# Two-layer hybrid decoder trunk on one core: layer 1's first heads put between the products of the query projections, early weight loads in halves, and turns moved in both output projections

## The chip, the cores and the metric

The kernel runs on one core of one Trainium2 chip. The metric is device time in microseconds (us), from runs of the whole kernel; smaller is better. A core has five engines that work through their own instruction streams in order and wait for each other through semaphores: TensorE (PE; its weight loads are listed as PEld), VectorE (DVE), ScalarE (ACT), GpSimd (POOL) and SyncE (SP). SP issues nearly all of the loads of this kernel. PSUM, where PE writes, is handed out in banks of 128 x 512 float32.

## The reference

The input is 256 tokens of 1024 channels, float32. Two layers follow each other, with a shared key/value step between them:

```python
hn = rms_norm(h, norm_gain[0, 0])                       # layer 0
h = h + stick_breaking_attention(hn, sb_w_qkv, sb_w_o)  # 16 heads of 64
h = h + sqrelu_mlp(rms_norm(h, norm_gain[0, 1]), w1, w2)  # 1024 -> 4096 -> 1024
shared = nsa_shared_kv(h, ...)     # one K/V projection for three branches
hn = rms_norm(h, norm_gain[1, 0])                       # layer 1
h = h + nsa_attention(hn, w_q, gate_b, w_o, shared)
h = h + sqrelu_mlp(rms_norm(h, norm_gain[1, 1]), w1, w2)
return rms_norm(h, final_norm)
```

Stick-breaking attention weighs a key by exp(log_sigmoid(z) + a reversed cumulative sum of log_sigmoid(-z)). The attention of layer 1 has 16 query heads in four groups that share keys and values. Each head is answered three times: over 15 compressed blocks (their keys and values come from a small MLP with 256 hidden units over 32 tokens each), over selected blocks of 64 tokens (with 256 tokens there are four blocks, all of which are selected, so this is causal attention), and over a window of 512 (causal attention again). The first 16 channels of queries and keys are rotated by position for the last two. Three sigmoid gates per head, columns of the query projection, weigh the three answers; their sum goes through the output projection.

## The kernel before

**Products.** Every large product is done in three passes of reduced-width float32 (`mm3`, lines 131 to 134, and `wide`, lines 139 to 145): each operand is split into a high part and the rest. Weights come through one stream: `feed` lists the tiles in the order of use, `fetch` (76) issues the next load into one of three `raw` buffers, and `split` (86) makes a high part `wh` on ACT (line 96) and a low part `wl` on DVE (line 97), each for half a tile at a time. `W(i)` makes sure that tile i is split, `step()` splits one more half, at most two tiles ahead. A load is issued when the second half of an earlier tile has been split. Most tiles are 128 x 2048 float32, 1 MB; the value projection of layer 0 is cut by `V_CUT` into six tiles: four with one block of 128 channels (512 KB), two with two blocks (1 MB). The first tile's load is two DMAs, one for each half of its columns.

**Layer 0.** The value projection (`v_proj`) goes block by block, as weights and input columns (`x_load`, `x_cut`) come in. Then eight query-key pairs (`proj`) run, with the attention of earlier pairs inside: `scores` (PE, then exponential, logarithm, scan, subtraction, and an exponential in line 432), `turn` (transposes in line 442, copies), `values`. The attention of the last pairs stands inside the output projection: `out_proj` takes a dictionary of steps that it calls at (i, n, kk), where i is the half of the 1024 input channels, n the half of the output columns (one weight tile for each i and n) and kk the block of 128 channels in that tile. A block of one tile is six products.

**Layer 1** (`nsa`, 470). `kv_proj` 0 to 2 make the keys and values of the three branches; `rope` (519) rotates on POOL in four instructions, for one tile of 128 tokens at a time; `keys_tr` transposes the keys; `cw_proj` is the first product of the compressing MLP, lines 612 to 623 its activation `hu`. `q_proj` (628) makes the queries in three parts (4, 6 and 6 heads, the gates with the first), each from two weight tiles with 24 products each; `mid` is called between the two tiles. `q_unrot` transposes unrotated queries for the compressed branch, `q_rope` rotates and splits, `q_rot` transposes the rotated ones. `cmp_kv` and `cmp_kv2` finish the compressed keys and values, `cmp_probs` makes compressed softmax weights for eight heads (one token tile after the other), `cmp_tr` transposes them. For each head, `scores` makes both branches' scores and exponentials, `scale` multiplies them on POOL by gate over sum, `turn` transposes, and `values` makes the answer of two heads. Lines 822 to 871 set the order: between the two tiles of parts 1 and 2 stand the transposes and rotation of the part before; after part 2, with no projection beside them, the scores of heads 1 to 3 and the rest of the preparation; then a loop over the heads, and the output projection with the last `values` inside.

**Order.** The order in which the source issues work is a priority. The order in each engine's stream is fixed at build time from it and from the expected readiness of inputs and buffers, so that a step can stand earlier or later than in the source. Tiles of one tag share a number of buffers: `bank` and `bank2` are two tags of four PSUM banks each, and a projection of layer 1 holds two of the first four.

## Time and profile before

| | |
|---|---|
| median of 3 runs | 640.27 us (639.65 to 640.73) |
| profiled execution | 642.27 us |
| its span, first to last instruction | 640.4 us |
| mean granted clock of PE | 0.999 |
| PE busy | 624.8 us (98%) |
| DVE busy | 435.6 us (68%) |
| ACT busy | 350.5 us (55%) |
| POOL busy | 59.6 us (9%) |
| weight subtractions on DVE, line 97 | 204, mean 1187 ns |
| weight casts on ACT, line 96 | 204, mean 1016 ns |
| HBM read | 106.22 MB |
| chain that ended last | PE 75%, DVE 12%, ACT 4%, DMA 4%, issue 3% |

A line of the timeline has the start from the span's start, the duration, engine, source line, operation, what is written from what, and in brackets the idle time before it and what ended it. Products overlap: one that is listed with 0.33 us can be followed by the next one 0.17 us later, and the busy time of PE counts the union. Layer 0 takes until about 122 us, its MLP until 302, the key/value step and layer 1's attention until 455, the last MLP the rest.

### The profile page before, as it was taken

The numbers are of one execution on the slowest core, as the hardware profiler recorded it, in microseconds if no ns is written. First come the engines' busy times: TensorE is split into PE (matmuls) and PEld (weight loads), VectorE is DVE, ScalarE is ACT, GpSimd is POOL, SyncE is SP. The second block draws the span as 40 slices with busy tenths as digits, with TensorE's granted clock in tenths as the row PEclk, the third lists the DMA queues.
The fourth block names the chain that finished last, engine by engine and source line by source line (L and its number), as shares of the span: only waits on it lengthen the run. The fifth ranks groups of instructions, "written<-read, shape, count | busy, mean of one in ns | idle before, by whom it ended". The sixth has DMA issues, their size and how long they took to land.

```text
span 640.4 us, 9068 instructions
## 1 busy us (share of the span) xinstructions
PE 624.8 (98%) x3541; PEld 527.9 (82%) x3541; DVE 435.6 (68%) x632; ACT 350.5 (55%) x606; POOL 59.6 (9%) x100
## 2 busy tenths in 40 slices
PE   9999999999999999999999999999999999999995
PEld 6799986888888888888889987777888888888884
DVE  5587887776566665666899879763776566666554
ACT  5666665464444544444847777752564544454433
POOL 0200000000000000000133344550000000000000
PEclk9999999999999999999999999999999999999999
DMA  8953333446555454553465742001545454555501
GB/s 264 409 211 133 132 132 121 151 174 212 197 182 206 160 208 169 201 190 133 150 253 192 258 156 98 3 2 66 198 168 205 162 204 182 198 198 197 198 0 67
DMA packets 17467, 107.86 MB, mean 168 GB/s; under 512 B 2320, under 2 KB 3088, under 8 KB 5648
## 3 DMA queue, kind: packets, MB, share of 16 engines
q1 hardware_dynamic: 16416, 106.03, 46.6%
q10 hardware_dynamic: 1008, 1.25, 0.5%
q8 instruction: 28, 0.46, 0.3%
q14 instruction: 15, 0.12, 0.1%
HBM read 106.22 MB, written 1.05 MB: 168 GB/s over the span
## 4 chain that ended last, share of the span: by engine, by line
PE 75%; DVE 12%; ACT 4%; DMA 4%; issue 3%; POOL 1%; SPq 0%; POOLq 0%; ACTq 0%; DVEq 0%
PE pu L137 27%; PE acc L132 11%; PE acc L133 11%; PE acc L134 11%; DVE wl L97 5%; PE po L137 2%; DMA raw<-in_wv 2%; DVE sbs L430 2%; PE pk L134 2%; PE pk L132 2%; PE pk L133 2%; ACT wh L96 1%; DVE sbe L424 1%; ACT sbs L429 1%; ACT sbs L428 1%
## 5 line engine op out<-in xcount | busy, mean ns | idle before, releaser
L97 DVE TENSOR_TENSOR wl<-raw,wh 128x1024 fp32r<-128x1024 f32 (+3 forms) x204 | 235.1, 1187 | 125.3 <-ACT wh L96 125.1
L96 ACT CAST wh<-raw 128x1024 fp32r<-128x1024 f32 (+3 forms) x204 | 198.5, 1016 | 118.2 <-PE acc L134 50.9
L137 PE MATMUL pu<-xn,wh 128*128 128x512 f32 x512 | 130.1, 392 | 0.6 <-DVE xn L204 0.6
L137 PEld LDWEIGHTS pu<-xn,wh 128*128 128x128 f32 x512 | 93.8, 188 | 19.6 <-DVE xn L204 1.8
L132 PE MATMUL acc<-wh,hh 128*128 128x512 f32 x256 | 100.2, 391 | 0.0
L133 PE MATMUL acc<-wl,hh 128*128 128x512 f32 x256 | 100.1, 391 | 0.0
L134 PE MATMUL acc<-wh,hl 128*128 128x512 f32 x256 | 99.5, 389 | 0.0
L137 PEld LDWEIGHTS pu<-xn,wl 128*128 128x128 f32 x512 | 71.0, 190 | 5.0
L137 PE MATMUL pu<-xn,wl 128*128 128x256 f32 x512 | 74.0, 282 | 0.0
L134 PEld LDWEIGHTS acc<-wh,hl 128*128 128x128 f32 x256 | 48.1, 188 | 10.6 <-DVE hl L293 0.4
L132 PEld LDWEIGHTS acc<-wh,hh 128*128 128x128 f32 x256 | 48.2, 188 | 9.6 <-ACT hh L292 0.6
L133 PEld LDWEIGHTS acc<-wl,hh 128*128 128x128 f32 x256 | 48.2, 188 | 8.8
L292 ACT CAST hh<-ms 128x512 fp32r<-128x512 f32 x32 | 19.9, 620 | 64.7 <-DVE ms L288 64.7
L286 ACT COPY mr<-pu 128x256 f32<-128x256 f32 x64 | 23.6, 369 | 29.2 <-PE pu L137 29.2
L132 PE MATMUL qk<-xa,wh 128*128 128x256 f32 x128 | 37.0, 289 | 0.0
L133 PE MATMUL qk<-xa,wh 128*128 128x256 f32 x128 | 36.2, 283 | 0.0
L134 PE MATMUL qk<-xa,wl 128*128 128x256 f32 x128 | 36.2, 283 | 0.0
L293 DVE TENSOR_TENSOR hl<-ms,hh 128x512 fp32r<-128x512 f32 x32 | 22.1, 692 | 19.9 <-ACT hh L292 19.9
L287 DVE TENSOR_TENSOR mu<-pu,mr 128x256 f32<-128x256 f32 x64 | 26.7, 418 | 5.8 <-ACT mr L286 5.8
L790 POOL TENSOR_TENSOR pe<-pe,rs 128x256 f32<-128x256 f32 (+1 forms) x32 | 27.1, 866 | 23.6 <-DVE rs L786 19.9
L132 PE MATMUL acc<-wh,oT 128*128 128x512 f32 x64 | 25.8, 403 | 0.0
L132 PEld LDWEIGHTS qk<-xa,wh 128*128 128x128 f32 x128 | 24.5, 191 | 1.0 <-issue 0.9
(187 smaller groups left out, 919.7 us busy)
## 6 DMA issues: line engine op xcount, KB each, us to landing
raw<-in_w SPq DMA_DIRECT2D x64, 1024.0 KB, 4.8
raw<-in_wqk SPq DMA_DIRECT2D x8, 1024.0 KB, 6.5
raw<-in_wo SPq DMA_DIRECT2D x8, 1024.0 KB, 4.8
raw<-in_wkv SPq DMA_DIRECT2D x6, 1024.0 KB, 4.8
raw<-in_cw SPq DMA_DIRECT2D x4, 1024.0 KB, 4.8
raw<-in_wv SPq DMA_DIRECT2D x2, 1024.0 KB, 8.1
raw<-in_wv SPq DMA_DIRECT2D x3, 512.0 KB, 5.6
raw<-in_wqb SPq DMA_DIRECT2D x2, 768.0 KB, 4.1
```

The source lines that it names most:

```text
L96: nc.scalar.copy(h[:, r], raws[j][:, r])
L97: nc.vector.tensor_sub(lo[:, r], raws[j][:, r], f32(h[:, r]))
L132: nc.tensor.matmul(o, a[0], b[0], start=first, stop=False, skip_group_check=True)
L133: nc.tensor.matmul(o, a[0], b[1], start=False, stop=False, skip_group_check=True)
L134: nc.tensor.matmul(o, a[1], b[0], start=False, stop=last, skip_group_check=True)
L137: nc.tensor.matmul(o, a, b, start=first, stop=last, skip_group_check=True)
L286: nc.scalar.copy(r[:, q], pu[f][:, 256:512])
L287: nc.vector.tensor_add(u[:, q], pu[f][:, 0:256], r[:, q])
L292: nc.scalar.copy(hh, sv)
L293: nc.vector.tensor_sub(hl, sv, f32(hh))
L430: nc.vector.tensor_tensor_scan(s[:, ::-1], s[:, ::-1], go_on[:, ::-1], 0.0, OP.add, OP.mult)
L790: nc.gpsimd.tensor_tensor(s, s, rs[:, t, :][:, :, None].to_broadcast([P, 2, n]), op=OP.mult)
```

## The change

Seven edits, in the order of the file. `fetch` makes two DMAs of each of the first seven loads (before: of the first alone). In layer 0's output projection `turn(NP - 2)` moves from (0, 0, 2) to (0, 1, 0) and `values(NP - 2)` from (0, 1, 1) to (0, 1, 2). `rope` takes both token tiles in its four instructions. `q_proj` takes a dictionary of steps by (i, kk) in place of `mid`, keeps both token tiles in one tile `q`, and makes the gates of both in one set of instructions. `cmp_probs` does the softmax of both token tiles together, from one PSUM bank. The last `values` of layer 1 writes a bank of the other tag. And the order of layer 1 is rewritten:

```diff
@@ fetch
-            if len(raws) == 1:
+            if len(raws) <= len(V_CUT) + 1:
@@ layer0
-        out_proj(oT, i_o0, {(0, 0, 2): [lambda: scores(NP - 1), lambda: turn(NP - 2), lambda: values(NP - 3)],
-                            (0, 1, 1): [lambda: values(NP - 2)],
+        out_proj(oT, i_o0, {(0, 0, 2): [lambda: scores(NP - 1), lambda: values(NP - 3)],
+                            (0, 1, 0): [lambda: turn(NP - 2)], (0, 1, 2): [lambda: values(NP - 2)],
@@ nsa
-        def rope(src, t, n):
...
+        def rope(src, n):
+
+            a = ap.tile([P, T, n, 16], F32, name="ropea", tag="ropea")
+            b = ap.tile([P, T, n, 16], F32, name="ropeb", tag="ropeb")
+            nc.gpsimd.tensor_mul(a, src[:, :, :, 0:16], cos[:, :, None, :].to_broadcast([P, T, n, 16]))
+            nc.gpsimd.tensor_mul(b[:, :, :, 0:8], src[:, :, :, 8:16], sin[:, :, None, 0:8].to_broadcast([P, T, n, 8]))
+            nc.gpsimd.tensor_mul(b[:, :, :, 8:16], src[:, :, :, 0:8], sin[:, :, None, 8:16].to_broadcast([P, T, n, 8]))
+            nc.gpsimd.tensor_add(src[:, :, :, 0:16], a, b)
...
-        def q_proj(n, mid=None):
+        def q_proj(n, hooks):
...
-                if i and mid is not None:
-                    mid()
                 for kk in range(4):
                     if kk % 2 == 0:
                         step()
+                    for f in hooks.get((i, kk), ()):
+                        f()
...
         def cmp_probs(hf):
+            pc = bank("psc")
             for t in range(T):
-                pc = bank("psc")
...
+            n = 8 * T
+            pv = pc[:, 0:T * 120].rearrange("p (h n) -> p h n", h=n)
...
-            po = bank("po1")
+            po = bank2("po1") if p == NP - 1 else bank("po1")
...
-        q1 = q_proj(1, after_q0)
-        q_rot(r[0], 0, 4)
-        cmp_kv2(*r.pop(1))
...
+        def turned(n, p0, np_, nh):
+            q_unrot(qn[n], p0, np_)
+            r[n] = q_rope(qn[n], nh)
+
+
+        qn[1] = q_proj(1, {(0, 1): [lambda: turned(0, 0, 2, 4)], (0, 2): [lambda: r.append(cmp_kv())],
+                           (1, 0): [lambda: q_rot(r[0], 0, 4)], (1, 1): [lambda: cmp_kv2(*r.pop())],
+                           (1, 2): [lambda: scores(0)]})
         qs[1] = big([P, NH // 2, T * P], F32R, "qs1")
-        scale(0)
-        scores(1)
-        q_rot(r[1], 4, 6)
-        q_unrot(q2, 5, 3)
-        r.append(q_rope(q2, 6))
-        cmp_probs(0)
-        scores(2)
-        scale(1)
-        turn(0)
-        cmp_tr(0)
-        q_rot(r[2], 10, 6)
+        qn[2] = q_proj(2, {(0, 1): [lambda: turned(1, 2, 3, 6), lambda: scores(1)], (0, 2): [lambda: scale(0)],
+                           (0, 3): [lambda: scores(2), lambda: scale(1)], (1, 0): [lambda: turn(0)],
+                           (1, 1): [lambda: q_rot(r[1], 4, 6), lambda: cmp_probs(0)],
+                           (1, 2): [lambda: turn(1), lambda: scale(2)], (1, 3): [lambda: scores(3)]})
...
-        scores(3)
-        scale(2)
-        turn(1)
-        cmp_probs(1)
-        for h in range(3, NH + 1):
+        cmp_tr(0)
+        for h in range(3, NH):
             if h + 1 < NH:
                 scores(h + 1)
-            if h < NH:
-                scale(h)
+            scale(h)
+            if h == 3:
+                turned(2, 5, 3, 6)
             if h % 2:
                 values((h - 3) // 2)
             turn(h - 1)
+            if h == 4:
+                q_rot(r[2], 10, 6)
+            if h == 5:
+                cmp_probs(1)
             if h == 6:
                 cmp_tr(1)
         xn = xt_tiles("n")
-        out_proj(oT, i_o1, {(0, 0, 2): [lambda: values(NP - 1)], (1, 1, 2): [lambda: xt_evac(xt_tr(0), 0, 3, xn)]})
+        out_proj(oT, i_o1, {(0, 0, 1): [lambda: turn(NH - 1)], (0, 0, 3): [lambda: values(NP - 1)], (1, 1, 2): [lambda: xt_evac(xt_tr(0), 0, 3, xn)]})
```

## Rows read from the trace of the kernel before

**Rows 1.** Waits of PE: who waited for whom, us in total, times, longest.
```profile
PE pv L132 <- ACT wh L96: 1.5, 1, 1.5
PE z L137 <- ACT pe L775: 1.4, 2, 0.7
PE pa L442 <- ACT sbe L432: 1.1, 2, 0.8
...
PE pct L745 <- DVE ce L737: 0.8, 1, 0.8
```

**Rows 2.** Stretches: length, then busy PE, PEld, DVE, ACT, POOL, clock, DMA.
```profile
354.20:376.70 22.50, 21.77 (x147) 20.88 (x146) 16.91 (x34) 13.60 (x27) 8.86 (x17) 1.00 0.62 222
376.70:392.00 15.30, 13.01 (x102) 10.56 (x102) 13.87 (x37) 14.06 (x49) 8.64 (x14) 1.00 0.18 70
```

**Rows 3.** Timeline of the first 20 us: PE, ACT, SP.
```profile
17.57 0.39 PE L134 MATMUL pv<-wh,xa 128*128 128x512 f32 x1
19.46 1.19 PE L132 MATMUL pv<-wh,xa 128*128 128x512 f32 x4 [1.50 <-ACT wh L96]
...
18.37 2.00 ACT L96 CAST wh<-raw 128x1024 fp32r<-128x1024 f32 x2 [2.70 <-DMA raw<-in_wv]
...
7.38 0.43 SPq L336 DMA_DIRECT2D xin<-in_xcols  x1
```

**Rows 4.** DMA issues from 0 to 40 us: count, KB each, us to landing.
```profile
raw<-in_wv SPq DMA_DIRECT2D x2, 1024.0 KB, 8.1
...
xin<-in_xcols SPq DMA_DIRECT2D x1, 512.0 KB, 6.6
```

**Rows 5.** Stretches as in group 2; the last number is GB/s.
```profile
4.00:6.00 2.00, 2.00 (x6) 0.75 (x5) 0.71 (x2) 1.36 (x3) 0.00 (x0) 1.00 0.98 245
...
12.00:14.00 2.00, 2.00 (x11) 1.65 (x10) 0.84 (x2) 1.19 (x3) 0.00 (x0) 1.00 0.96 328
```

**Rows 6.** Timeline of layer 0's output projection, ACT and PE.
```profile
97.25 0.85 ACT L432 ACTIVATE sbe<-sbe 128x774 f32<-128x774 f32 x1 [1.40 <-DVE sbe L431]
...
98.15 0.88 PE L442 MATMUL pa<-ident,sbe 128*128 128x128 f32 x6 [0.80 <-ACT sbe L432]
```

**Rows 7.** Timeline of the second query projection's first half, PE and DVE.
```profile
354.23 0.34 PE L132 MATMUL pq<-wh,xq 128*128 128x384 f32 x1
...
358.39 0.60 PE L660 MATMUL ptq<-ident,q 128*128 128x128 f32 x4
359.32 0.45 PE L693 MATMUL pht<-ident,hu 60*128 60x60 f32 x4 [0.33 <-DVE hu L623]
...
358.64 0.62 DVE L623 TENSOR_TENSOR hu<-hu,hx 60x512 f32<-60x512 f32 x1
```

**Rows 8.** Timeline of PE in the stretch of the first heads.
```profile
383.35 0.22 PE L137 MATMUL psc<-cmb,cbf 128*128 128x120 bf16 x1
383.37 0.36 PE L137 MATMUL z<-kT,qs 128*128 128x256 f32 x1
```

**Rows 9.** Timeline of the second key branch's rotation: POOL, DVE, PE.
```profile
339.24 1.33 POOL L524 TENSOR_TENSOR ropea<-kd,cst 128x128 f32<-128x128 f32 x1
...
343.17 0.46 POOL L529 TENSOR_TENSOR kd<-ropea,ropeb 128x128 f32<-128x128 f32 x1
...
338.78 4.13 DVE L97 TENSOR_TENSOR wl<-raw,wh 128x1024 fp32r<-128x1024 f32 x3
...
341.85 0.60 PE L573 MATMUL ptk<-ident,kd 128*128 128x128 f32 x4
...
343.68 0.66 PE L573 MATMUL ptk<-ident,kd 128*128 128x128 f32 x4 [0.87 <-POOL kd L529]
```

**Rows 10.** Query evacuations on DVE (timeline), and the page's group of the scaling.
```profile
354.43 0.53 DVE L480 TENSOR_SCALAR q<-pq,r 128x304 f32<-128x304 f32 x1
364.92 0.61 DVE L480 TENSOR_SCALAR q<-pq,r 128x384 f32<-128x384 f32 x1
...
L790 POOL TENSOR_TENSOR pe<-pe,rs 128x256 f32<-128x256 f32 (+1 forms) x32 | 27.1, 866 | 23.6 <-DVE rs L786 19.9
```

More of the change, by code (lines that the diff above doesn't have):

```diff
@@ L565, in keys_rope @@
         def keys_rope(br):
-            for t in range(T):
-                rope(kd[br][t].rearrange("p g a d -> p (g a) d"), t, 2 * NG)
+            rope(kdt[:, br].rearrange("p t (h d) -> p t h d", d=DH), 2 * NG)
         def keys_tr(br):
@@ L626, in nsa @@
         gates = ap.tile([P, T, 48], F32, name="gates")
-        def q_proj(n, mid=None):
+        def q_proj(n, hooks):
             cn = 384 if n else 304
-            qn = [ap.tile([P, 384], F32, name=f"q{t}", bufs=2)[:, 0:cn] for t in range(T)]
+            qn = ap.tile([P, T, 384], F32, name="q", bufs=2)
             pq = [bank(f"pq{t}") for t in range(T)]
@@ L642, in q_proj @@
             for t in range(T):
-                evac(qn[t], pq[t][:, 0:cn], t)
+                evac(qn[:, t, 0:cn], pq[t][:, 0:cn], t)
             if n == 0:
-                for t in range(T):
-                    gt = gates[:, t, :]
-                    nc.vector.tensor_add(gt, qn[t][:, 256:304], gbs)
-                    nc.vector.tensor_scalar(gt, gt, -80.0, None, op0=OP.max)
-                    nc.scalar.activation(gt, gt, AF.Exp, scale=-1.0)
-                    nc.vector.tensor_scalar(gt, gt, 1.0, None, op0=OP.add)
-                    nc.vector.reciprocal(gt, gt)
+                nc.vector.tensor_add(gates, qn[:, :, 256:304], gbs[:, None, :].to_broadcast([P, T, 48]))
+                nc.vector.tensor_scalar(gates, gates, -80.0, None, op0=OP.max)
+                nc.scalar.activation(gates, gates, AF.Exp, scale=-1.0)
+                nc.vector.tensor_scalar(gates, gates, 1.0, None, op0=OP.add)
+                nc.vector.reciprocal(gates, gates)
+                nc.vector.tensor_tensor(gates[:, :, 0:NH], gates[:, :, 0:NH],
+                                        cst[:, C_ANY:C_ANY + T][:, :, None].to_broadcast([P, T, NH]), op=OP.mult)
             return qn
@@ L659, in q_unrot @@
                     for t in range(T):
[L660 removed]
+                        nc.tensor.transpose(pt[:, j, t * P:(t + 1) * P], qn[:, t, (a + j) * P:(a + j + 1) * P], ident)
                 nc.scalar.activation(qT[:, p0 + a:p0 + a + m, :], pt[:, 0:m, :], AF.Copy, scale=0.125)
         def q_rope(qn, nh):
[L664 removed]
+            qv = qn[:, :, 0:nh * DH].rearrange("p t (h d) -> p t h d", h=nh)
+            rope(qv, nh)
+            sp_ = ap.tile([P, T, 6, 2, DH], F32R, name="qsp")
+            qsp = [sp_[:, t, 0:nh] for t in range(T)]
             for t in range(T):
[L666 to L670 removed]
+                nc.scalar.activation(qsp[t][:, :, 0, :], qv[:, t], AF.Copy, scale=0.125)
+                nc.vector.scalar_tensor_tensor(qsp[t][:, :, 1, :], qv[:, t], 0.125, f32(qsp[t][:, :, 0, :]),
                                                op0=OP.mult, op1=OP.subtract)
[L672 removed]
             return qsp
@@ L737, in cmp_probs @@
-                nc.vector.tensor_tensor(e, e, sm[:, :, None].to_broadcast([P, 8, NC]), op=OP.mult)
-                live[hf, t] = e
+                    mm(pc[:, t * 120 + i * 30:t * 120 + (i + 1) * 30], qT[:, p, t * P:(t + 1) * P], kcb[:, p // 2, :],
+                       t == 0 and i == 0, False)
+            for t in range(T):
+                mm(pc[:, t * 120:(t + 1) * 120].rearrange("p (h n) -> p h n", h=8), ident_b,
+                   cmb[:, t * NC:(t + 1) * NC][:, None, :].to_broadcast([P, 8, NC]), False, True)
@@ new lines, in cmp_probs @@
+            n = 8 * T
+            pv = pc[:, 0:T * 120].rearrange("p (h n) -> p h n", h=n)
+            mx = ap.tile([P, n], F32, name="cmx")
+            nc.vector.tensor_reduce(mx, pv, axis=AX.X, op=OP.max)
+            e = ap.tile([P, n, NC], F32, name="ce", bufs=2)
+            nc.vector.tensor_tensor(e, pv, mx[:, :, None].to_broadcast([P, n, NC]), op=OP.subtract)
+            nc.scalar.activation(e, e, AF.Exp)
+            sm = ap.tile([P, n], F32, name="csm")
+            nc.vector.tensor_reduce(sm, e, axis=AX.X, op=OP.add)
```

52 lines of the change are left out of this document (9 added, 43 removed).

## The prediction, made before the changed kernel was run

> **What bounds the kernel now.** I read the page's totals first, then the list of what PE waited for, then the stretches of the three places that the diff touches. PE is busy in 98% of the span, so the span is PE's work plus PE's waits. The diff removes no product and no transpose (it joins vector and GpSimd instructions, but the 18 small products of each compressed-score step stay 18), so it can only give back waits. [rows 1] is the list of the waits that matter here: 1.5 us for the first weights, 1.1 us in layer 0's turn, and in layer 1 1.4 us of scores waiting for an exponential and 0.8 us of compressed transposes. With 0.9 us of key transposes [rows 9] and 0.3 us of hidden-unit transposes [rows 7] that is 6.0 us, 0.9% of the time, and about the ceiling of the change. [rows 2] tells where layer 1's waits sit: in the stretch with the second and third query projections PE is busy 21.77 of 22.50 us and DVE and ACT have room (16.91 and 13.60); in the next 15.3 us, where the first heads are started without products beside them, DVE is busy 13.87 and ACT 14.06 us and PE stands for 2.29. So the first heads' vector work comes in a lump behind the projections.
>
> **The change, part by part.**
>
> *The first loads in halves.* Loads 2 to 7 of the weight stream (five of the value projection, one of the first query-key pair) become two DMAs each; SP issues six more. In [rows 3] PE's last product of the fourth value block starts at 17.57 and the next one at 19.46, after 1.50 us of waiting for a cast that itself waited 2.70 us for a load of 1 MB. That load holds two blocks, and the cast goes by halves, so it needs the first 512 KB only. What stood ahead of it in the queue, the 512 KB of input columns issued at 7.38, takes 6.6 us by [rows 4], until 13.98; the 1 MB is there at 18.37. Spread evenly, its first half is there at (13.98 + 18.37)/2 = 16.2; a cast of 1.0 us makes 17.2, before PE is free. The second half comes at 18.37 as before, is cast by 19.4, and PE reaches it only after the first block's twelve products. So the whole 1.50 us can go. The low part of the first block, 1.2 us of DVE behind its cast, would be there at 18.4, behind four products that need the high part alone; the 0.1 us that I add for it is an estimate, and 0.3 its most (four products of 0.23 us, the width of the columns taken from [rows 7], against the 1.2 us of subtraction). Best end: -1.8. For the other end the price of smaller pieces isn't in the trace as such; nearest are the two stretches of [rows 5]: 245 GB/s at 4 to 6 us, when 256 KB halves and 128 KB columns were moving, and 328 GB/s at 12 to 14, with 512 KB and 1 MB loads. If halves move at the first rate, the 3.67 MB of loads 2 to 6 take 15.0 instead of 11.2 us, 3.8 us later; of that the head start of the first half (2.2 us) comes off, so +1.6. I take -1.6, near the best end, because the bytes, the queue and their order are the same and only the landing of the first half is asked for.
>
> The Trainium skill, "DMA: Bandwidth & Descriptors", section "Bandwidth", asks for 1 MiB and more in one DMA and gives 341 GB/s there against 138 at 64 KB. [rows 4] agrees so far that 512 KB take 6.6 us and 1 MB 8.1, not twice as long. By that rule the term would be the +1.6 and the sum that of the second rival.
>
> *Layer 0's sixth turn, moved behind two more steps of the output projection.* [rows 6]: the exponential of that pair runs 97.25 to 98.10, and PE's transposes wait 0.80 us for it. Moved to the next weight tile, the turn has twelve products of 0.23 us, 2.8 us, and the values of pair 5 ahead of it; the wait goes, and values of pair 6 move by one step as well, so that a step's products still lie between its copies and its use. Late next would be the last pair's exponential, because the two copies of the moved turn now fall among the last pair's activations on ACT; its own turn stands four steps, 24 products or 5.5 us, behind the moved one, so this costs nothing. -0.8; ends -0.8 and 0.
>
> *Layer 1, first heads between the products.* The scores of heads 0 to 3, two turns, the rotation's transposes and the first compressed scores now stand between the 96 products of query projections 1 and 2. What they waited for runs beside products. The two score waits (1.4) and the compressed transposes (0.8) are the ones with products as new cover: -2.2 if all of it goes, 0 if none. The moved heads' vector work goes from the second stretch of [rows 2] into the first; DVE over both is 30.8 of 37.8 us, so it fits, without much left.
>
> *Compressed hidden units, earlier.* Their transposes stood at the start of the second weight half and now stand two steps earlier. [rows 7]: the products begin at 354.23, 24 of them end at 358.39, the four query transposes take until about 359, and the hidden units come from DVE at 359.26, so PE waits 0.33. Two steps earlier is half of 4.16 us: 354.23 + 2.1 + 0.6 = 356.9. If PE's stream has the transposes there, it waits 2.4 us, 2.1 more than now. If the order is kept by readiness, nothing: [rows 8] show that an engine's order is not the source's (a score product of the next head stands between the compressed scores of a step that precedes it in the source). Ends -0.3 and +2.1; I take +0.5.
>
> *Rotation in one piece for both token tiles.* Four GpSimd instructions instead of eight, each twice as large. [rows 9]: for the second key branch the second token tile's rotation began at 339.24; its first instruction took 1.33 us while DVE ran three weight subtractions of 4.13 us together; the last, equal in size and free of that, took 0.46. The transposes of the first token tile were already issued at 341.85; those of the second waited 0.87 us. Joined, both tiles wait for one end. With 4 x 0.92 (twice 0.46) from 339.24 that is 342.9 (wait 1.1 at the first transposes, none at the second: +0.2); with four instructions at 1.33 it is 344.6 (2.7, so +1.9); started 0.7 us sooner, since both inputs stand ready before 339.24, and at 0.46 to 0.9 each, the wait is gone: -0.9. I take 0.
>
> *Joined gate, compressed softmax and copy instructions; the last turn and values inside the output projection; the last values in the other PSUM tag.* These make DVE's and ACT's instructions fewer, behind PE's products, and take nothing off PE. With that cover gone they would be worth what the lump stretch has left of PE's 2.29 us when the two waits above are gone, 0.1; here 0. The last turn gains a step's products as cover and its own values another two; 0.
>
> Sum: -1.6 - 0.8 - 2.2 + 0.5 + 0 = -4.1 us. Against the profiled execution, 642.27 us (span 640.4 and 1.9 around it), this is 638.2; the median of the timed runs lies 2.0 under that execution, so I forecast **636.2 us**. After each of the three places PE has its products back to back, with weights ahead, so what is given back there should arrive at the end.
>
> **The rivals.**
>
> *The wait only moves (637.8).* For it: the hidden units come at 359.26 whatever PE does, and DVE keeps its 30.8 us. Then layer 1 gives -2.2 + 2.1 = -0.1, and with the -2.4 of the two other places -2.5 remain. Against it: [rows 8]. The same time comes out if the first half of a load lands with the second (the change would not do what it says): the start's -1.6 is gone, -2.5, 637.8.
>
> *Halves slow the stream (639.4).* Start +1.6, the rest -2.5: -0.9. Against it: DMA is not what PE waits for before 16 us.
>
> *All of it goes (634.3).* -1.8 - 0.8 - 2.2 - 0.3 - 0.9 = -6.0. For it: each of these has products beside it in the new order. Against it: the keys' rotation has no new cover.
>
> *GpSimd becomes the bound in the query projections: slower (643.0).* Its rotation runs beside the weight subtractions, at 1.33 us an instruction in [rows 9], and now stands ahead of the first heads' scaling in GpSimd's queue, while PE's rotation transposes and first turn stand behind it. Keys: +1.9. Query part 0: both tiles are evacuated at 355.0 [rows 10], 4 x 1.33 makes 360.3, and its transposes are due four products' steps, four query and four hidden transposes after 354.23, at 359.4; with the cast and subtraction between still to come, +1.5 (0.9 without them). Part 1: the second tile is evacuated 1.5 us after the third projection's first products could start (365.5 against 364.0 for the end of the second), 5.3 us of rotation and 2 x 0.87 of scaling follow: 8.5; the first turn is due after 24 products, six transposes and two heads' scores, 4.2 + 0.7 + 1.9 = 6.8: +1.7. With these the heads run as late as now and the 2.2 stays: +5.1 - 2.4 = +2.7. It decides from about 3.7 us of such waits on (then the total is above +1.3). Against it: the rotation is in part free of the subtractions, and its instructions are fewer.
> The Trainium skill, "SBUF — State Buffer", section "Who interferes with whom", has this as a lock: a DVE instruction with two SBUF inputs and a GpSimd instruction that reads SBUF exclude each other for a whole instruction. [rows 9] agree, 1.33 against 0.46 us; by that rule a wait is paid per instruction, which speaks for four instructions and against this rival.
>
> **How the numbers follow.** Forecast 0.50 (its own range 634.8 to 637.5), all of it 0.12, the wait moves or the halves land together 0.21, halves slow 0.10, GpSimd 0.07. A measurement of this kernel can tell about 0.2%, 1.3 us, from no change. Faster by more than that (under 639.0): 0.50 + 0.12 + 0.21 = 0.83; same: 0.10; slower: 0.07. The range goes down to 633.0, that 1.3 us under the case in which all of it goes, and up to 639.6; it leaves out the slow case, half of the halves' and some 0.02 below, 0.14 together.
>
> **What would show it.** The value products of the fifth block start near 17.9 us with no wait for a cast; layer 0's transposes stand 2.7 us or more behind the exponential; PE's waits under score and compressed transposes in layer 1 are under 0.5 us in sum; the wait of the hidden-unit transposes is under 1 us; key transposes wait about 0.9. Wrong: the start moves by less than 0.8 us, PE's busy share in the query projections falls, or waits for GpSimd's rotation or scaling stand at the head of PE's list.

## The result: slower, and the profile after

The changed kernel takes 644.38 us (median of 10 runs, 642.38 to 649.8) against 640.50 us for the kernel before on the same chip: ratio 1.0067, 95% interval 1.0042 to 1.0093. Forecast were 636.2 us, with 0.83 on faster. The profiled execution took 647.29 us (span 645.4, mean granted clock 0.989), so it is the second slowest of the ten.

The list of what PE waited for in the changed kernel answers to [rows 1], [rows 7] and [rows 9] (columns as there):
```profile
PE ptk L569 <- POOL kd L526: 1.9, 1, 1.9
PE ptr L676 <- DVE rs L786: 1.9, 1, 1.9
PE pct L745 <- DVE ce L737: 1.3, 1, 1.3
...
PE pa L442 <- ACT sbe L432: 0.7, 1, 0.7
...
PE pht L689 <- DVE hu L619: 0.6, 1, 0.6
...
PE z L137 <- ACT pe L775: 0.4, 1, 0.4
```
The wait for the first weights is gone, layer 0's turn has one wait of 0.7 us left of two, and the scores of layer 1 wait 0.4 in place of 1.4 us. But the key transposes wait 1.9 instead of 0.9, the compressed transposes 1.3 instead of 0.8, and there is a new wait of 1.9 us under `ptr`, the transposes of rotated queries. A wait for GpSimd's rotation stands at the head of the list, one of the signs that the prediction named for being wrong.

The stretches of the changed kernel from the second to the end of the third query projection answer to [rows 2], with the same columns; the number to read is the granted clock, third from the end:
```profile
354.00:376.00 22.00, 20.56 (x140) 18.47 (x138) 16.47 (x33) 13.92 (x37) 8.74 (x11) 1.00 0.42 153
376.00:380.00 4.00, 2.88 (x19) 2.51 (x19) 3.69 (x9) 4.00 (x12) 2.75 (x3) 0.87 0.72 270
380.00:384.00 4.00, 4.00 (x21) 4.00 (x20) 1.41 (x2) 0.70 (x2) 2.30 (x2) 0.50 0.36 109
384.00:388.00 4.00, 4.00 (x18) 3.48 (x18) 2.03 (x5) 0.43 (x2) 0.00 (x0) 0.50 0.37 154
388.00:392.00 4.00, 4.00 (x25) 3.34 (x24) 3.35 (x11) 3.32 (x11) 1.24 (x3) 0.85 0.01 2
```
Before, the clock was 1.00 in all of this. PE's busy share in the first stretch fell too, from 97% of [rows 2] (21.77 of 22.50) to 93%, another sign that the prediction named. Then the clock is at the lower level, 1.2 GHz, for some ten microseconds while PE is busy throughout and DVE and ACT run dry: (0.13 + 0.50 + 0.50 + 0.15) x 4 = 5.1 us of PE's time. That is the most that the fall can have cost here: part of it PE would have spent waiting.

What PE did before the fall stands in the timeline of that place:
```profile
374.79 0.34 PE L134 MATMUL pq<-wh,xq 128*128 128x384 f32 x1
377.01 0.51 PE L676 MATMUL ptr<-ident_r,qsp 128*128 128x128 f32 x4 [1.89 <-DVE rs L786]
...
376.34 0.53 DVE L803 COPY pT<-ptp 128x384 f32<-128x384 f32 x1
...
378.18 0.51 ACT L805 COPY pT<-ptp 128x384 f32<-128x384 f32 x1
...
380.85 3.45 PE L137 MATMUL psc<-kcb,qTu 128*128 128x30 f32 x16
```
The wait is put down to DVE's `rs`, but that is only DVE's last event before it. The transposes need a bank of the tag of which the projection holds two and the first turn's transposes the other two; those are copied out by DVE at 376.34 and by ACT at 378.18, behind a weight subtraction and a weight cast, the scores' maxima and eight exponentials. DVE's copy ends at 376.87, and the first transposes start 0.14 us later.

PE's milestones in the two profiled executions give the balance. The first product of layer 0's MLP starts 2.26 us earlier (122.65 to 120.39). From the first compressing product to the first query product it takes 11.34 instead of 10.31 us (+1.03, the keys); from there to the output projection 88.50 instead of 82.86 (+5.64); the output projection takes 0.68 more, because the last turn now stands inside. The sum, +5.09, is the shift of PE's last product (5.06) to a rounding. The last two of these stages together, before and after:
```profile
347.55:455.51 107.96, 104.23 (x702) 85.74 (x701) 79.06 (x182) 65.97 (x200) 39.38 (x57) 1.00 0.32 114
346.32:460.60 114.28, 108.69 (x702) 89.12 (x701) 78.56 (x166) 65.89 (x197) 37.77 (x45) 0.96 0.29 106
```
PE stands for 5.59 us instead of 3.73 (+1.9), and it is busy for 4.5 us longer with the same products, at the lower clock.

Not every execution loses as much: the ten had mean clocks of 0.986 to 0.998. The two at 0.998 took 642.38 and 643.06 us; the one at 0.986 took 649.80. The shortest fall in layer 1 of any trace here lasts 3.4 us (e9_tile_rope), which by itself takes 0.0027 off the mean; so (an estimate) an execution at 0.998 or more had no such fall. Without one, then, the changed kernel still loses about 2 us.

### The profile page after: what moved, and what is told of

Its sections match the earlier page's. It is cut to its first block, busy times and chain, and to the rows that moved or that the text cites. A ratio compares the mean times of both kernels' runs of the same rounds, so it can differ in the third digit from the quotient of the medians.

```text
span 645.4 us, 9025 instructions
## 1 busy us (share of the span) xinstructions
PE 628.5 (97%) x3541; PEld 531.3 (82%) x3541; DVE 436.7 (68%) x617; ACT 351.1 (54%) x603; POOL 55.6 (9%) x80
## 4 chain that ended last, share of the span: by engine, by line
PE 82%; DVE 8%; ACT 3%; issue 3%; POOL 2%; DMA 2%; POOLq 0%; ACTq 0%; DVEq 0%
PE pu L137 27%; PE acc L132 11%; PE acc L133 11%; PE acc L134 11%; PE po L137 3%; DVE wl L97 2%; PE z L137 2%; DMA raw<-in_wqk 2%; PE qk L132 1%; PE pk L134 1%; PE pk L132 1%; PE pk L133 1%; PE qk L133 1%; PE qk L134 1%; ACT wh L96 1%
```

## The experiments

Theory A: the third projection's steps starve PE of banks, and the clock falls after the wait. Rivals: the joined rotation (B), the loads (C), vector engines that are late whatever the banks (D). All were timed beside the kernel before, in groups on different chips; ratios are to the kernel before on the same chip, and differences between experiments are taken from the ratios.

**e1_front**: the kernel before with the loads in halves and layer 0's turn as changed, layer 1 as before.
```diff
-            if len(raws) == 1:
+            if len(raws) <= len(V_CUT) + 1:
...
-        ... [lambda: scores(NP - 1), lambda: turn(NP - 2), lambda: values(NP - 3)],
-                            (0, 1, 1): [lambda: values(NP - 2)],
+        ... [lambda: scores(NP - 1), lambda: values(NP - 3)],
+                            (0, 1, 0): [lambda: turn(NP - 2)], (0, 1, 2): [lambda: values(NP - 2)],
```


> The kernel before with only the loads of the first seven tiles in halves and layer 0's sixth turn moved; layer 1 as before. Theory A (the loss is made in layer 1, by the third query projection's steps and by the granted clock that falls after PE's wait there): the 2.3 us that the changed kernel has gained at the first product after layer 0 stay to the end, 638.2 us against 640.5, ratio 0.9964. Theory B (the joined rotation on GpSimd costs it): the same here, since it is not in. Theory C (the halves slow the load stream later): 640.5 or more. Granted clock 1.00 from 360 us to 400 us.

Measured: 640.03 us, ratio 0.9984 (0.9974 to 0.9995), clock 1.00 until the last few microseconds of the kernel. So the loss is in layer 1; but only 0.9 us of the 2.3 seen between two traces is kept.

**e12_halves**: the kernel before with the halves alone.
```diff
-            if len(raws) == 1:
+            if len(raws) <= len(V_CUT) + 1:
```


> The kernel before with only the loads of the first seven tiles in halves. By the traces, the first query and key product starts 2.2 to 2.7 us earlier and 0.9 us is given back in the pairs: if the profiled execution of before stands for the others, ratio 0.9975 to 0.9985; if its 1.5 us wait at the start was more than others have, 0.999 to 1.000.

Measured: 641.40 us, ratio 0.9998 (0.9988 to 1.0008). The halves bring nothing. The list of PE's waits of this execution shows new ones in place of [rows 1]'s first line:
```profile
PE z L137 <- DVE qkT L405: 0.8, 1, 0.8
...
PE pv L133 <- DVE wl L97: 0.8, 1, 0.8
```
The weights' low parts are late at the start, and in the second pair the scores wait for a product that they did not wait for before. Together they are as long as the wait that went, and in this trace layer 0's MLP starts only 0.4 us earlier (122.29 against 122.65). Layer 0's turn is then the rest, 0.9998 to 0.9984 or 0.9 us; the two intervals overlap.

**e16_pair**: e1_front, first scores of layer 0 at the same block as in the other pairs.
```diff
-            return {2 if n == 1 else 5: [...
+            return {5: [...
```


> e1_front with the first scores of layer 0 put three blocks later in the second pair's projection (at the same block as in the other pairs), where e1_front's trace has a wait of 0.5 us for the pair's queries and keys, other executions up to 1.2 us. If that wait is paid: it goes, 0.5 to 1.0 us less than e1_front, ratio 0.997. If the work only moves: as e1_front within 0.3 us, ratio 0.998 to 0.999.

Measured: 639.52 us, ratio 0.9985 (0.9973 to 0.9997). The wait for `qkT` is gone from the list and the time is e1_front's: that wait was not paid. With e1_front this is the fastest kernel of the study; both beat the kernel before and the changed one.

**e2_rot_bank**: the changed kernel, second group's transposes in the scores' tag.
```diff
-                pt = bank("ptr", F32R)
+                pt = ps.tile([P, 512], F32R, tag="z", name="ptr", bufs=4) if z else bank("ptr", F32R)
```


> The changed kernel, but the second group of rotated queries is transposed into three banks of the tag that the scores use. Theory A (these transposes wait for a bank of the tag that the projection itself holds two of): the 2.2 us wait on a bank ahead of them goes or falls under 0.5 us, the granted clock stays at 1.00 between 378 us and 390 us, and the kernel takes about 638 to 640 us, 4 to 6 us less than the changed one (ratio to before 0.996 to 0.999). Theory D (the vector engines are too far behind whatever bank is used): the wait moves to the next transposes or scores, the clock still falls, and the time stays at 643 to 645 us.

Measured: 649.17 us, ratio 1.0127 (1.0112 to 1.0143). The timeline of PE, and the stretches behind it:
```profile
382.26 0.28 PE L676 MATMUL ptr<-ident_r,qsp 128*128 128x128 f32 x1 [1.33 <-ACT pe L775]
```
```profile
380.00:384.00 4.00, 2.51 (x19) 2.23 (x18) 3.97 (x9) 4.00 (x15) 2.33 (x2) 0.86 0.72 246
384.00:388.00 4.00, 4.00 (x18) 3.95 (x18) 0.96 (x3) 1.60 (x3) 1.74 (x3) 0.50 0.07 25
```
The first two tiles no longer wait; the third does, for a bank that an exponential on ACT still reads. Another bank for these transposes does not cure it, which speaks for D; but the time is above what either theory said, and the edit takes banks from the scores, so it does not separate the two cleanly. (Its profiled execution also loses 3 us at the start, where PE waited 2.2 us for weights and the clock fell to 0.50 behind it; the edit does not touch that.)

**e8_scores_only**: the changed kernel, both turns and the compressed scores moved behind the third projection.
```diff
-                           (0, 3): [lambda: scores(2), lambda: scale(1)], (1, 0): [lambda: turn(0)],
-                           (1, 1): [lambda: q_rot(r[1], 4, 6), lambda: cmp_probs(0)],
-                           (1, 2): [lambda: turn(1), lambda: scale(2)], (1, 3): [lambda: scores(3)]})
+                           (0, 3): [lambda: scores(2), lambda: scale(1)],
+                           (1, 1): [lambda: q_rot(r[1], 4, 6)],
+                           (1, 2): [lambda: scale(2)], (1, 3): [lambda: scores(3)]})
+        cmp_probs(0)
+        turn(0)
+        turn(1)
```


> The changed kernel with both turns and the compressed scores of the first eight heads moved from within the third projection to behind it; scores, scaling and the second group's transposes stay inside. Theory A (the transposes starve of banks because the turn's two banks are copied late): the 1.9 us wait ahead of the second group's transposes falls under 0.5 us and the clock stays at 1.00 there; 640 to 642 us. Theory D (ACT and DVE are too far behind whatever the banks): a wait of over 1 us on scores or transposes stays within the projection, with the clock at 0.5 behind it, and the time is 643 us or more.

Measured: 648.07 us, ratio 1.0113 (1.0096 to 1.0129). PE's timeline:
```profile
381.57 0.28 PE L676 MATMUL ptr<-ident_r,qsp 128*128 128x128 f32 x1 [2.07 <-DVE qs L682]
...
397.89 0.33 PE L799 MATMUL ptp<-ident,pe 128*128 128x128 f32 x1 [2.58 <-ACT pT L805]
```
With the turns and the compressed scores gone from the tag (the projection still holds two of its four banks), the transposes wait for the copies of their own group, and the turns behind the projection for theirs. A wait of over 1 us and a time over 643 us are what D said; that the clock falls behind the wait is not: it stayed at 1.00 there and fell at 344 and 398 us. So late copies remain the better account, but that four banks are too few is not excluded.

**e6_after_third**: the changed kernel, all steps of the third projection but the unrotated transposes and the rotation put behind it.
```diff
-        qn[2] = q_proj(2, {(0, 1): [lambda: turned(1, 2, 3, 6), lambda: scores(1)], ...
+        qn[2] = q_proj(2, {(1, 0): [lambda: turned(1, 2, 3, 6)]})
+        scores(1)
+        scale(0)
...
+        turn(1)
```


> The changed kernel, with the steps of the third query projection taken out of its later products: the second group's transposes and rotation between its two tiles as before, scores, turns and compressed scores right after it; the second projection's steps, the loop over the heads and the output projection stay as changed. Theory A: the 2.2 us wait inside the third projection and the fall of the clock from 378 us to 390 us are gone, PE stands some 2 to 3 us after the projection instead as the kernel before did, and the time is 640 to 641.5 us, 3 to 4 us under the changed kernel (ratio to before 0.999 to 1.001). Rival E (the loss comes of the new loop over the heads): 643 us or more.

Measured: 645.38 us, ratio 1.0058 (1.0038 to 1.0079). PE stands behind the projection instead, 1.5 us at most under a turn, and the clock falls at 340 to 348 us (0.78 and 0.80) and at 396 to 400 (0.60). Where the steps of the third projection stand is not the whole cause. Rival E, the new loop over the heads, was never tested apart; its time (643 us or more) came, and two of this trace's waits, 1.47 us under the turn and 0.63 under the last group's `ptr`, lie in that loop.

**e3_rope_tile**: the changed kernel with `rope` for one token tile at a time.
```diff
-            rope(qv, nh)
...
+                rope(qv[:, t], t, nh)
```


> The changed kernel with the rotation done for one token tile at a time again, in keys and queries. Theory A: PE's 1.9 us wait of the key transposes for GpSimd shrinks by about 1.0 us, the wait ahead of the second group's transposes and the fall of the clock stay: 643.4 us (ratio to before 1.0045). Theory B (the joined rotation is the main cause): 639 to 641 us, no fall of the clock.

Measured: 644.27 us, ratio 1.0075 (1.0049 to 1.0101). PE's timeline at the keys and in the third projection:
```profile
342.66 0.33 PE L573 MATMUL ptk<-ident,kd 128*128 128x128 f32 x1 [0.89 <-POOL kd L529]
...
378.36 0.25 PE L680 MATMUL ptr<-ident_r,qsp 128*128 128x128 f32 x1 [2.54 <-DVE rs L790]
```
The key transposes get their 1.0 us back, `ptr` waits 0.65 us longer, and nothing remains. B is out as the main cause.

**e4_fill**: the changed kernel with eight zero products of 512 columns ahead of `ptr`.
```diff
-                           (1, 1): [lambda: q_rot(r[1], 4, 6), ...
+                           (1, 1): [lambda: fill(8), lambda: q_rot(r[1], 4, 6), ...
```


> The changed kernel with eight products of zeros (bf16, 128x512, 0.21 us each at the full clock, estimated from the 0.63 us that such a product takes at the start of the kernel at the low clock) put ahead of the second group's transposes, where PE stands for 2.2 us; they add 1.7 us of work that nothing reads. If the fall of the clock is made by PE's standing there: the work fits into the wait, the clock stays up, and the time falls by about 4 us, to 640 to 641 us. If the fall comes of something else: 644.4 us or up to 1.7 us more, with the clock at 0.5 from 380 us to 388 us.

Measured: 646.85 us, ratio 1.0092 (1.0070 to 1.0114). The clock stays at 1.00 to 380 us, but the second `ptr` tile then waits 1.29 us and it falls to 0.75 and 0.50. The fall was put off, not avoided, so on the clock this is inconclusive. But three of the six executions had a mean clock of 0.998 or 0.999, no room for a fall, and still took 644.91 to 646.07 us; the added products take about 1.8 us in the trace. Over 2 us of loss are there without any fall.

**e5_joined, e9_tile_rope, e7_one_head**: layer 1's old order in the changed kernel; the same without the joined rotation; e5_joined with one head's scores between the last products.
```diff
+        qn[1] = q_proj(1, {(1, 0): [after_q0]})
...
-        qn[2] = q_proj(2, {(1, 0): [after_q1]})
+        qn[2] = q_proj(2, {(1, 0): [after_q1], (1, 3): [lambda: scores(1), lambda: scale(0)]})
...
-        scale(0)
-        scores(1)
```
(The first added line is in all three, the rest in e7_one_head.)

> The changed kernel with layer 1's old order (one group of steps between the two tiles of the second and of the third query projection, the rest after them, last turn ahead of the output projection) but all joined instructions: rotation, gates and compressed softmax of both token tiles at once. Theory A (the order, above all the steps within the third projection, makes the loss): about 640.5 us, that is e1_front's ratio 0.9984 and up to 1.0 us of the key transposes' wait, ratio 0.998 to 1.000, and no fall of the clock from 360 us to 400 us. Theory B (the joined instructions): 642 us or more, ratio over 1.002.

> e5_joined (layer 1's old order with all joined instructions, ratio 1.0046) with the rotation of one token tile at a time again; gates and compressed softmax stay joined. If the joined rotation makes e5_joined's loss: the key transposes wait 0.9 us in place of 1.9, the clock stays at 1.00 from 340 us to 348 us and from 384 us to 396 us, ratio 0.998 to 1.000 as e1_front. If the joined softmax does: the 2.9 us wait of the scores near 387 us stays, with the clock at 0.5 behind it, and the ratio is 1.002 to 1.004.

> e5_joined with one thing more: the scores of head 1 and the scaling of head 0 between the last products of the third projection, where they take two banks of the scores' tag and none of the other. If scores alone are worth putting between products, it takes 0.7 to 1.4 us less than e5_joined (the score waits of the kernel before, 1.4 us), no fall of the clock. If the vector engines are the bound of that whole stretch: as e5_joined within 0.5 us.

Measured: 643.96 us, ratio 1.0046 (1.0031 to 1.0062); 644.73 us, 1.0047 (1.0034 to 1.0061); 643.01 us, 1.0037 (1.0023 to 1.0050). This was the surprise: without any new order, with joined instructions, the kernel loses 4.0 us against e1_front, and the joined rotation has no part in it that the times show. In e5_joined PE waits 2.89 us near 387 us for the scores' bank, in e9_tile_rope 2.00, and the clock falls to 0.50 and 0.68 there. One head between products shortens e5_joined's wait to 1.61 us; the time is 1.0 us less, with intervals that overlap. e7_one_head's two executions at 0.998 and 0.999 took 641.27 and 640.96 us, under 1 us above the kernel before: here most of the loss comes with a lower clock.

**e13_softmax**: e1_front with the joined compressed softmax alone (and the one multiplication of the gates that goes with it).
```diff
-            for t in range(T):
-                pc = bank("psc")
+            pc = bank("psc")
+            for t in range(T):
...
+            n = 8 * T
+            pv = pc[:, 0:T * 120].rearrange("p (h n) -> p h n", h=n)
```


> e1_front with one thing of layer 1 changed: the compressed softmax of both token tiles joined, from one bank (with the factor for tokens without a block moved into the gates). e9_tile_rope, where softmax and gates are joined, stood 4.0 us above e1_front. If the joined softmax is the cause: the scores' wait of about 2 us near 387 us and a fall of the clock about it are back, ratio 1.002 to 1.005. If it is not: as e1_front, ratio 0.998 to 0.9995, and the cause of e9_tile_rope is in the joined gates or the query tile that holds both token tiles.

Measured: 644.22 us, ratio 1.0052 (1.0037 to 1.0068): alone 4.4 us above e1_front. That is as much as e9_tile_rope, which has the joined gates as well, so these cost nothing that shows. The stretches of e1_front (first) and of e13_softmax:
```profile
380.00:384.00 4.00, 3.33 (x30) 3.05 (x30) 3.19 (x8) 3.61 (x12) 3.56 (x7) 1.00 0.01 2
384.00:388.00 4.00, 3.22 (x26) 2.56 (x26) 3.93 (x17) 3.42 (x15) 0.00 (x0) 1.00 0.00 0
```
```profile
380.00:384.00 4.00, 4.00 (x26) 3.85 (x27) 1.92 (x6) 3.90 (x13) 1.66 (x5) 0.70 0.01 2
384.00:388.00 4.00, 3.07 (x13) 2.07 (x11) 3.32 (x8) 1.49 (x8) 1.61 (x2) 0.50 0.00 0
388.00:392.00 4.00, 3.39 (x12) 2.22 (x12) 4.00 (x11) 2.87 (x16) 2.59 (x2) 0.52 0.21 49
```
Their timelines, again e1_front first:
```profile
380.05 1.04 PE L137 MATMUL psc<-kcb,qTu 128*128 128x30 f32 x8
...
381.16 0.97 PE L137 MATMUL psc<-kcb,qTu 128*128 128x30 f32 x8
...
381.65 0.68 DVE L770 TENSOR_REDUCE nm<-z 128x2 f32<-128x512 f32 x1
```
```profile
379.32 0.50 PE L137 MATMUL z<-kT,qs 128*128 128x512 f32 x1 [0.72 <-ACT pe L781]
...
380.54 2.62 PE L137 MATMUL psc<-kcb,qTu 128*128 128x30 f32 x16
...
385.16 1.35 DVE L672 SCALAR_TENSOR_TENSOR qsp<-q,qsp 128x384 fp32r<-128x384 f32 x2
386.44 0.40 DVE L736 TENSOR_TENSOR ce<-psc,cmx 128x240 f32<-128x240 f32 x1
386.75 0.41 DVE L777 TENSOR_REDUCE nm<-z 128x2 f32<-128x256 f32 x1
...
388.61 1.22 PE L137 MATMUL z<-kT,qs 128*128 128x512 f32 x2 [1.54 <-ACT pe L781]
```
Apart, the narrow products come in two groups of eight, with score products between. Joined, all sixteen come in one piece, and the clock falls within them, after a stand of only 0.72 us. The scores that stood between them come later, their maximum (386.75) stands behind the split of the last queries on DVE, and PE waits 1.54 us for the bank.

**e17_softmax_fill, e18_front_fill**: eight zero products among the narrow ones, in e13_softmax and in e1_front.
```diff
+                    if hf == 0:
+                        mm(pc[:, 256:512], zero[:, 0:P], zero[:, 0:256], False, True)
```


> e13_softmax (ratio 1.0052) with a product of zeros, 128x256 in bf16, put behind each of the eight narrow compressed products of the first half of the heads, into the unused half of their bank; nothing reads it. At the full clock that adds 8 x 0.11 = 0.9 us of PE work. If the fall of the clock about 380 us to 392 us follows on PE's narrow products and stands and is most of the loss: the clock there stays at or near 1.00 and the time falls in spite of the added work, ratio 1.001 to 1.003. If the loss is the joined softmax's longer chain: the fall may go or not, the ratio stays at 1.005 or rises to 1.0065.

> e1_front with the same eight products of zeros, as the measure of what they cost where the clock does not fall: 0 to 0.9 us more than e1_front's ratio 0.9984, that is 0.9984 to 1.000.

Measured: 642.61 us, ratio 1.0027 (1.0018 to 1.0036), and 641.61 us, ratio 1.0012 (0.9994 to 1.0031). The stretches of e17_softmax_fill:
```profile
380.00:384.00 4.00, 3.04 (x34) 2.79 (x32) 3.16 (x5) 2.63 (x10) 3.92 (x6) 1.00 0.28 84
384.00:388.00 4.00, 2.82 (x13) 1.59 (x13) 4.00 (x13) 4.00 (x20) 0.97 (x3) 1.00 0.44 180
388.00:392.00 4.00, 3.34 (x27) 2.72 (x28) 3.91 (x11) 1.99 (x7) 3.56 (x5) 1.00 0.00 0
```
More work on PE, of which nothing is used, made the kernel 1.6 us faster, and the two intervals just do not meet. PE's work stands in the same order in both traces. The clock stays up although PE still stands (its scores wait 1.06 us at the longest). So 1.6 us of the 4.4, and what the products themselves cost, are the clock.

What they cost, e18_front_fill does not measure cleanly. By the ratios it is 1.8 us, and the clock's share would be 3.4; but with the products in it the scores no longer stand between the two groups, and PE waits for their bank longer than e1_front's 0.67 us, at a clock of 1.00:
```profile
387.08 0.73 PE L137 MATMUL z<-kT,qs 128*128 128x512 f32 x2 [2.01 <-ACT pe L777]
```
Also its executions have lower mean clocks than e1_front's (median 0.995 against 0.998). The traces give another measure, from the first query product to the last MLP, for e1_front, e18_front_fill, e17_softmax_fill and e13_softmax:
```profile
345.01:453.08 108.07, 104.23 (x703) 85.76 (x701) 79.03 (x182) 66.05 (x200) 39.60 (x57) 1.00 0.33 114
345.76:454.13 108.37, 104.20 (x710) 85.75 (x709) 79.32 (x182) 66.01 (x200) 39.17 (x57) 1.00 0.32 114
345.13:455.39 110.26, 105.53 (x710) 86.22 (x709) 78.24 (x171) 65.89 (x198) 39.09 (x57) 1.00 0.31 112
345.70:457.65 111.95, 108.31 (x702) 88.61 (x701) 78.19 (x171) 66.01 (x198) 39.04 (x57) 0.95 0.31 109
```
Here the products cost 0.3 us and the fall 1.7 to 2.0 of 3.9 us. The slow clock adds 4.1 us to PE's busy time (108.31 against 104.23), but with the clock up about 1 us of it comes back as waits (4.73 instead of 3.64 us). The clock's share of the 4.4 us is thus between 1.6 and 3.4; the rest is the longer chain.

**e10_front_head**: e1_front with one head's scores between the third projection's last products.
```diff
+                    if late is not None and i and kk == 3:
+                        late()
...
-        scale(0)
-        scores(1)
```


> e1_front (nothing joined) with the scores of head 1 and the scaling of head 0 between the last products of the third projection instead of behind it. e7_one_head took 1.0 us less than e5_joined by the same step. If that was a wait of the scores that goes: 0.4 to 1.0 us less than e1_front, ratio 0.997 to 0.998. If it only shortened a wait that e1_front has not: ratio 0.998 to 1.000.

Measured: 643.40 us, ratio 1.0035 (1.0019 to 1.0050), 3.3 us above e1_front. PE's timeline:
```profile
377.86 0.28 PE L682 MATMUL ptr<-ident_r,qsp 128*128 128x128 f32 x1 [0.97 <-DVE q L480]
...
385.51 0.50 PE L137 MATMUL z<-kT,qs 128*128 128x512 f32 x1 [1.66 <-ACT pe L777]
```
The two score waits of 0.7 us become others of 0.97 and 1.66: this reads as work behind the projection that is short of DVE and ACT, not of a better order on PE. In this profile the clock holds; in five of the ten executions its mean is at 0.995 or less.

**e14_order_rope, e15_order_alone**: the changed kernel with the softmax by token tile; that with the rotation by token tile as well.
```diff
-            pc = bank("psc")
             for t in range(T):
+                pc = bank("psc")
...
-            rope(qv, nh)
```
(The last line in e15_order_alone.)

> The changed kernel with the compressed softmax of one token tile at a time again; order and rotation as changed. If the joined softmax makes most of the changed kernel's loss: about 4 us under it, 640 to 641 us, ratio 0.999 to 1.001, no fall of the clock between 378 us and 390 us. If the new order does: the wait ahead of the second group's transposes and the fall stay, ratio 1.005 or more.

> The changed kernel with softmax and rotation of one token tile at a time again: of layer 1's edits only the order, the joined gates and the last answer's bank are left. If the order by itself costs: ratio 1.004 or more, with a wait of over 1.5 us inside the third projection and the clock at 0.5 behind it. If order and joined instructions only hurt together: ratio 0.997 to 1.000.

Measured: 644.50 us, ratio 1.0070 (1.0049 to 1.0092); 646.88 us, ratio 1.0103 (1.0070 to 1.0135), its six executions from 644.36 to 650.80. The wait of `ptr` is 1.91 and 2.65 us, with the clock at 0.50 from 380 to 388 us in both. For e15_order_alone:
```profile
377.88 0.51 PE L677 MATMUL ptr<-ident_r,qsp 128*128 128x128 f32 x4 [2.65 <-DVE rs L783]
```
The new order loses by itself, as much as the whole change. The losses do not add; that this is because each makes the same stretch late is not shown.

**e11_pool_1us**: e1_front with a GpSimd instruction of the first key branch done twice.
```diff
             nc.gpsimd.tensor_mul(a, src[:, :, 0:16], c)
+            if again:
+                nc.gpsimd.tensor_mul(a, src[:, :, 0:16], c)
```


> e1_front with one rotation instruction of each token tile of the first key branch done twice on GpSimd (0.5 to 1.3 us each, 1 to 2 us in the chain that the key transposes wait for); nothing joined, PE's order there unchanged. If a wait of PE is paid as such: 1 to 2 us more than e1_front, clock at 1.00 from 340 us to 348 us. If a wait of about 2 us there makes the granted clock fall, as the traces of the joined kernels show at that place: 2.5 to 4 us more, ratio 1.002 to 1.005, clock under 0.9 from 340 us to 348 us and a mean clock of 0.993 to 0.996 in most executions.

Measured: 640.62 us, ratio 0.9990 (0.9977 to 1.0003), the wait 0.89 us as ever. A miss: that wait belongs to the second key branch, and the first has slack. It tells nothing of the clock.

## Why the prediction was wrong

*The first loads in halves (-1.6).* The wait for the cast is gone from the traces, the gain is not in the time (e12_halves). The step that failed is "So the whole 1.50 us can go": the wait for the low part, put at 0.1 us and 0.3 at most, measures 0.76 in e12_halves, and one of 0.81 for the second pair's queries and keys was not looked for. The rival that halves slow the stream did not come true either, 393 GB/s at 12 to 14 us in the changed kernel against 328 in [rows 5]. The Trainium skill, "DMA: Bandwidth & Descriptors", section "Bandwidth", asks for 1 MiB and more; here pieces of 256 and 512 KB cost nothing that the times show (ratio 0.9998).

*Layer 0's sixth turn (-0.8).* Right: the last pair's end to the MLP takes 28.25 instead of 29.18 us, and e1_front against e12_halves gives 0.9, with intervals that overlap.

*Layer 1, first heads between the products (-2.2).* This step failed most: forecast between -2.2 and 0, the order alone stands 7.6 us above e1_front (with joined gates in it). With it the premise failed that a diff without new products "can only give back waits": in the changed kernel's trace PE waits 1.9 us more in this stage and its products take 4.5 us longer. It read room from [rows 2], DVE 16.91 and ACT 13.60 of 22.50 us, and added DVE's busy time over both stretches. But busy time is no room where PE waits for one copy in a queue: in the trace above the copies that free the banks stand behind a weight split, maxima and eight exponentials, and PE's transposes start when the first copy is done. The score waits went as forecast; a wait of 1.9 us under `ptr` took their place, the one question the step did not ask ("what stands ahead of the copy that frees the bank?"). Other or fewer users of the banks did not cure it (e2_rot_bank, e8_scores_only). In the kernels with the new order the executions at a mean clock of 0.998 or more stand at 642.4 to 644.6 us (e4_fill, with its added products, at 644.9 to 646.1), 2 to 4 us above the kernel before: these are waits. The rest comes with the lower clock.

*Joined gate and compressed softmax (0).* "The 18 small products of each compressed-score step stay 18" was right and beside the point. They come in one piece, that alone costs 4.4 us (e13_softmax), 1.6 to 3.4 of it through the clock (e17_softmax_fill). The clock was at 1.00 in all rows and the prediction took it as given.
The Trainium skill, "TensorE: Matmul & The Clock Gate", section "A second HAM failure mode: psum-queue depth-cycling", tells of a kernel in which short pauses between groups of products made the clock go down and up; e13_softmax agrees so far that no pause over 0.72 us stands ahead of its fall. But e17_softmax_fill has the same pause and no fall, so here the pause alone is not the cause.

*Rotation in one piece (0, ends -0.9 and +1.9).* +1.0 at the keys, inside the bounds: in one piece the last instruction ends at 341.59, and the first tile's transposes, which before were issued without a wait [rows 9], wait for it too. In the changed kernel's time it does not show (e3_rope_tile).

*Hidden-unit transposes (+0.5).* 0.57 us instead of 0.33: +0.2, right.

*The rival "GpSimd becomes the bound" (643.0)* came nearest in time and not in mechanism: with the rotation by tile the wait in the third projection is longer (e3_rope_tile), and behind the split queries PE waits only 0.5 us.

Not settled: why the fall comes in some executions and not in others of the same kernel; which part of the new order, the steps in the third projection or the loop over the heads, makes the waits; and how the changed kernel's loss divides to a tenth. Of the 3.9 us, about 2 stand without a fall (the two executions at 0.998); the rest in the median, and up to 7 us in the slowest execution, comes with a lower clock.

## What to carry to other kernels

In a stretch where DVE was busy three quarters of the time and ACT 60%, moving their work under products traded one wait for another; ask what stands ahead of the copy that frees each bank, not how busy its engine is on average. Look at how narrow products come: on this kernel sixteen in a row brought the clock down where two groups of eight, with score products between, did not, and joining them saved nothing that shows. Ask also whether a diff can lower the clock, not only what waits it gives back. Read a gain at the start of a kernel from timed runs, since a wait that goes can come back a step later, as it did in e12_halves.

## What the hardware showed unexpectedly

The granted clock fell to 1.2 GHz after PE had stood for 0.72 us and gone on with sixteen narrow products (e13_softmax), in other kernels about or after stands of 1.3 to 2.9 us, once after two of 0.96 and 0.67 us (e15_order_alone, at 400 us), and stayed there for 3 to 10 us, with PE busy for most of them. A stand of this length need not bring a fall: the clock stayed at 1.00 behind 1.66 us in e10_front_head, 2.01 in e18_front_fill and 2.07 in e8_scores_only. Behind the keys' 1.9 us wait it fell in four of the eight profiles that have this wait (to 0.50 in e5_joined), and stayed at 1.00 in the others, the changed kernel's among them. And a low clock is not paid in full: in e13_softmax it lengthened PE's busy time by 4.1 us, and without the fall (e17_softmax_fill) 1.7 us came back.
